# Edge blocks of a windowed attention, widened from 192 keys to 256 with zero weights

## The chip, the cores and the metric

One Trainium2 chip, one core of it. The metric is the device time of one execution in microseconds (us), the median of several runs. Below, PE is the matrix engine (TensorE) and PEld its loads of the stationary operand, DVE is VectorE, ACT is ScalarE, POOL is GpSimd and SP is SyncE, which issues most transfers.

## The reference

The program is one layer of a bidirectional encoder, on two requests of 256 and 2048 rows with width 1024. After a normalization and one input projection, the columns go two ways: 512 channels through a gated long convolution (Hyena, by Fourier transforms) and 8 heads of 64 through a dilated sliding-window attention. Both are normalized, joined, projected and added; a gated feed-forward network follows. The attention is what matters here:

```python
DILATED_BRANCHES = ((128, 1), (512, 4), (2048, 16))   # window, dilation
R = window // (2 * dilation)                          # 64 in all three
rel = jnp.arange(W)[None, :] - R - jnp.arange(b)[:, None]
valid = (jnp.abs(rel) <= R)[None] & ((key_pos >= 0) & (key_pos < Ls))[:, None, :]
s = jnp.where(valid, s + bias, NEG_INF)
p = jnp.exp(s - m)                                    # m: the row's maximum
den = jnp.sum(p, axis=-1)
o = jnp.einsum('brnhqk,brnkhe->brnqhe', p, v) / den
```

Each query sees the keys at most 64 steps (of the dilation) to either side, and a key in front of the sequence or behind it does not count. The three branches are then merged by their softmax denominators.

## The kernel before

The work is float32 throughout. Projections, the output product and the feed-forward network take three products of rounded halves each (the helper `mm3`, lines 208 to 210); attention and Hyena are woven into one stage, from about 985 to 1656 us of the profiled execution. The functions are generators: each `yield` hands the turn to the other one, and `weave` takes the one that is behind its share (the shares stand in `RATES`). That gives the order of the program. A scheduler then orders the instructions of each engine at build time, and each engine runs its list in that order.

`attention` goes over four pairs of heads, three branches for each, and the groups of blocks of `attention_groups`. A block is 128 queries of one pair of heads against its keys, and it takes four steps:

- `scores` (lines 906 and 907): two products for each head into the PSUM tile `aS`; then DVE adds the bias and takes the row's minimum (line 910; the sign is turned in the scores), and ACT takes the exponential (line 913), both on `aP`, a tile with two buffers.
- `flip` (line 922): PE transposes the weights `aP`, 128 keys at a time, into `aT`; the copy to `aPT` is made by DVE for each third block and by ACT for the others (line 926, or line 929 where the parts are not both 128 keys).
- `values` (line 938): for each head and part, the product of `aPT` and the values `aV`, summed in `aOp`. A column of ones beside the values gives the denominator. Each such float32 product is two PE instructions in the trace.
- At the end of a group, ACT copies `aOp` to `aO` (line 942) and SP stores it.

There are 216 blocks. Inside a sequence a block sees 256 keys, in two parts of 128. At its two ends a block sees 192: the first block of a sequence in parts of 64 and 128 keys, the last in parts of 128 and 64. There are 48 of these edge blocks: for each pair of heads 2 and 2 in the branch of dilation 1 and 8 in that of dilation 4. The other blocks (dilation 16, and the short request in the dilated branches) have one part of 128 keys. So in an edge block the value products of one part have 64 rows, and the transposes of that part have 64 columns. `attention_values` (lines 813 to 846) loads the values of a branch: half a tile for the first 64 keys, whole tiles of 128, and half a tile for the last 64; POOL writes the ones first (line 820).

The Hyena steps that run between have their PE products on lines 692, 693, 723, 727, 741 and 778. The addition on POOL (line 735) takes what DVE made on lines 731 to 734, and line 741 multiplies its result.

Of the kernel before, what the change touches and what calls it, by code (L numbers as in the profile page):

```python
# [15 lines left out]
AF = mybir.ActivationFunctionType  # L16
# [5 lines left out]
P = 128  # L22
# [167 lines left out]
class Hybrid:  # L190
# [624 lines left out]
    def attention_values(self, wp, b, cs):  # L815

        nc = self.nc
        dil = DILS[b]
        vo = wp.tile([P, 22, 130], F32, tag="aV", name="aV", bufs=2)
        nc.gpsimd.memset(vo[:, :, 0:130:129], 1.0)  # L820
        vt = vo[:, :, 1:129]
        av = self.tok["av"][:, cs]
        ld = lambda o, i: nc.sync.dma_start(out=o, in_=i)
        base = {}
        n = 0
        for r in (1, 0):
            off, L = REQ[r]
            base[r] = n
            ls = L // dil
            if ls >= 256:  # L830
                nb = ls // P
                e = 64 * dil
                ld(vt[0:64, n:n + dil], av[off:off + e].rearrange("(p s) k -> p s k", s=dil))
                if dil == 1:
                    ld(vt[:, n + 1:n + nb], av[off + e:off + L - e].rearrange("(c p) k -> p c k", p=P))
                else:
                    for c in range(1, nb):
                        o2 = off + e + (c - 1) * P * dil
# [35 lines left out]
    def attention(self, wp, psS, psT, psO, first, mq):  # L874
        nc, a = self.nc, self.a
        q1, q2 = [], []

        def scores(heads, g, i, blk, ot, bias, b):
            r, kind, _ = g
            res, j, nb = blk  # L880
            dil = DILS[b]
            off, L = REQ[r]
            ps = psS.tile([P, 2, 256], F32, tag="aS", name="aS")
            sb = wp.tile([P, 2, 256], F32, tag="aP", name="aP", bufs=2)
            for hh in range(2):
                Ql, Ks, Qh = heads[hh]
                t0 = off + res + dil * P * j
                qs = slice(t0, t0 + dil * (P - 1) + 1, dil)
                if kind == "win":
                    qa, qb = Qh[:, qs], Ql[:, qs]  # L890
                    k0 = max(0, P * j - 64)
                    n = min(nb * P, P * j + 192) - k0
                    v0, N = 0, n
                    b0 = k0 - (P * j - 64)
                    m0 = off + res + dil * k0
                    rhs = Ks[:, m0:m0 + dil * (n - 1) + 1:dil]
                elif kind == "res":
                    qa, qb = Qh[:, qs], Ql[:, qs]
                    e = res - res % 2
                    rhs = Ks[:, off:off + L].rearrange("p (j s) -> p s j", s=dil)[:, e:e + 2]  # L900
                    v0, n, N, b0 = P * (res % 2), P, 256, 0
                else:
                    qa, qb = Qh[:, off + j:off + L:2], Ql[:, off + j:off + L:2]
                    rhs = Ks[:, off:off + L].rearrange("p (j s) -> p s j", s=2)
                    v0, n, N, b0 = P * j, P, 256, 256 if b == 1 else 128
                nc.tensor.matmul(ps[:, hh, :N], qa, rhs, start=True, stop=False)
                nc.tensor.matmul(ps[:, hh, :N], qb, rhs, start=False, stop=True)
            for hh in range(2):
                mn = ot[:, i, 130 + hh:131 + hh]
                nc.vector.tensor_tensor_reduce(out=sb[:, hh, :n], in0=ps[:, hh, v0:v0 + n],  # L910
                                               in1=bias[:, hh, b0:b0 + n], scale=1.0, scalar=3e38,
                                               op0=ALU.add, op1=ALU.min, accum_out=mn)
                nc.scalar.activation(sb[:, hh, :n], sb[:, hh, :n], AF.Exp, scale=-1.0, bias=mn)
            return sb, n

        def flip(x):
            sb, n, first = x["sb"], x["n"], x["first"]
            ch = [(0, 64), (64, 128)] if first else [(0, P)] + ([(P, n - P)] if n > P else [])
            pt = psT.tile([P, 2, 2, P], F32, tag="aT", name="aT")
            for hh in range(2):  # L920
                for c, (c0, cn) in enumerate(ch):
                    nc.tensor.transpose(pt[:cn, hh, c], sb[:, hh, c0:c0 + cn], self.ident)  # L922
            pe = wp.tile([P, 2, 2, P], F32, tag="aPT", name="aPT", bufs=3)
            eng = nc.vector.tensor_copy if x["k"] % 3 == 0 else nc.scalar.copy
            if all(cn == P for _, cn in ch):
                eng(pe[:, :, :len(ch)], pt[:, :, :len(ch)])
            else:
                for c, (c0, cn) in enumerate(ch):
                    eng(pe[:cn, :, c], pt[:cn, :, c])
            x["pe"], x["ch"] = pe, ch  # L930

        def values(x):

            po, vt, i, pe, ch = x["po"], x["vt"], x["i"], x["pe"], x["ch"]
            for hh in range(2):
                hs = slice(65 * hh, 65 * hh + 65)
                for c, (c0, cn) in enumerate(ch):
                    nc.tensor.matmul(po[:, i, hs], pe[:cn, hh, c], vt[:cn, x["v"] + c * x["vs"], hs],  # L938
                                     start=(c == 0), stop=(c == len(ch) - 1))
            if x["last"]:  # L940
                n = i + 1
                nc.scalar.copy(x["ot"][:, :n, 0:130], po[:, :n])  # L942
                x["store"]()
# [30 lines left out]
        k = 0  # L974
# [4 lines left out]
        for hp in range(4):  # L979
# [6 lines left out]
            for b in range(3):  # L986
                dil = DILS[b]
                lo = (0, 256, 640)[b]
                w = (256, 384, 256)[b]
                bias = wp.tile([P, 2, 384], F32, tag="aB", name="aB", bufs=2)  # L990
                nc.sync.dma_start(out=bias[:, :, :w], in_=a["abias"][:, 2 * hp:2 * hp + 2, lo:lo + w])
                vt, vbase = self.attention_values(wp, b, cs)
                for g in self.attention_groups(b, (0, 1) if hp == 3 else (1, 0)):
                    r, kind, blks = g
                    ot = wp.tile([P, G, W], F32, tag="aO", name="aO", bufs=4)
                    po = psO.tile([P, G, 130], F32, tag="aOp", name="aOp")
                    for i, blk in enumerate(blks):
                        res, j, nb = blk
                        if hp == 0:
                            next(own, None)  # L1000
                        sb, n = scores(heads, g, i, blk, ot, bias, b)
                        x = dict(sb=sb, n=n, first=(kind == "win" and j == 0), k=k, po=po, vt=vt, i=i, ot=ot,
                                 last=(i == len(blks) - 1), store=store(b, hp, g, ot))
                        if kind == "win":
                            x["v"], x["vs"] = vbase[r] + j * dil + res, dil
# [680 lines left out]
```

## Time and profile before

| | |
|---|---|
| median of 3 runs | 3516.02 us (3508.4 to 3517.49) |
| the profiled execution | 3503.98 us |
| its span, first to last instruction | 3502.1 us |
| mean granted clock of TensorE | 0.970 |
| stage of attention and Hyena | 985 to 1656 us |
| the edge blocks' value products with 64 rows | 192 PE instructions |
| the edge blocks' transposes with 64 columns | 96 |

A row of the trace names the line, the engine and the operation, the tile written and the tiles read, and the shapes. For PE, `64*128` means that 64 rows and 128 columns of the array are in use. "Idle before" is the time in which the engine had nothing running ahead of these instructions, with what ended it. Products on PE overlap: the next one starts before the last has ended, so the time that one takes on PE is the distance from its start to the next start, not its length.

### The profile page before, as it was taken

The numbers are of one execution on the slowest core, as the hardware profiler recorded it, in microseconds if no ns is written. First come the engines' busy times: TensorE is split into PE (matmuls) and PEld (weight loads), VectorE is DVE, ScalarE is ACT, GpSimd is POOL, SyncE is SP. The second block draws the span as 40 slices with busy tenths as digits, with TensorE's granted clock in tenths as the row PEclk, the third lists the DMA queues.
The fourth block names the chain that finished last, engine by engine and source line by source line (L and its number), as shares of the span: only waits on it lengthen the run. The fifth ranks groups of instructions, "written<-read, shape, count | busy, mean of one in ns | idle before, by whom it ended". The sixth has DMA issues, their size and how long they took to land.

```text
span 3502.1 us, 56839 instructions
## 1 busy us (share of the span) xinstructions
PE 3290.7 (94%) x20926; PEld 3020.3 (86%) x20926; DVE 2461.5 (70%) x4254; ACT 1560.1 (45%) x2922; POOL 1267.1 (36%) x946
## 2 busy tenths in 40 slices
PE   7999899999989999999799899999999999899998
PEld 4877788788857786778799799999899999899998
DVE  7989878776575658644887766667767667457657
ACT  4576743333244545455554433334333334344443
POOL 1487761142232413110444433334533335123222
PEclk9999999999999999998999899999999999999999
DMA  6454457776585857593676523445444224456555
GB/s 244 133 169 135 148 182 234 238 263 219 177 246 160 243 163 216 157 272 106 185 225 184 193 96 122 145 158 187 179 158 146 85 95 148 173 190 229 206 190 172
DMA packets 408909, 628.02 MB, mean 179 GB/s; under 512 B 29007, under 2 KB 232015, under 8 KB 402711
## 3 DMA queue, kind: packets, MB, share of 16 engines
q1 hardware_dynamic: 355472, 593.13, 52.1%
q10 hardware_dynamic: 52072, 28.40, 2.7%
q8 instruction: 166, 2.72, 0.3%
q0 software_dynamic: 1088, 2.85, 0.2%
q14 instruction: 111, 0.91, 0.1%
HBM read 419.03 MB, written 205.25 MB: 178 GB/s over the span
## 4 chain that ended last, share of the span: by engine, by line
PE 42%; DVE 5%; DMA 2%; issue 2%; ACT 1%; POOL 1%; ACTq 0%; SPq 0%; DVEq 0%; POOLq 0%
PE w L210 9%; PE w L208 9%; PE w L209 9%; PE fd L210 4%; PE fd L209 4%; PE fd L208 4%; DVE fT L1251 1%; DMA hl<-d_opT 0%; DMA d_x1T<-ox 0%; DVE ohy L1159 0%; DVE ox L1214 0%; DVE hl L203 0%; POOL oat L1145 0%; PE om L208 0%; PE om L210 0%
## 5 line engine op out<-in xcount | busy, mean ns | idle before, releaser
L208 PE MATMUL w<-hh,whi 128*128 128x288 f32 (+1 forms) x2464 | 737.3, 300 | 13.1 <-ACT whi L1345 8.3
L210 PE MATMUL w<-hh,wlo 128*128 128x290 f32 (+1 forms) x2464 | 734.2, 299 | 13.7 <-POOL wlo L203 10.1
L209 PE MATMUL w<-hl,whi 128*128 128x288 f32 (+1 forms) x2464 | 737.2, 300 | 3.3 <-DVE hl L203 3.2
L210 PEld LDWEIGHTS w<-hh,wlo 128*128 128x128 f32 x2464 | 471.5, 192 | 15.7 <-POOL wlo L203 11.2
L208 PEld LDWEIGHTS w<-hh,whi 128*128 128x128 f32 x2464 | 472.2, 192 | 14.9 <-ACT whi L1345 8.6
L209 PEld LDWEIGHTS w<-hl,whi 128*128 128x128 f32 x2464 | 474.0, 192 | 4.6 <-DVE hl L203 4.4
L208 PE MATMUL pj<-hThi,wihi 128*128 128x386 f32 (+1 forms) x1152 | 403.4, 351 | 12.6 <-ACT u L629 5.2
L209 PE MATMUL pj<-hTlo,wihi 128*128 128x386 f32 (+1 forms) x1152 | 401.0, 348 | 7.4 <-DVE hTlo L203 7.4
L210 PE MATMUL pj<-hThi,wilo 128*128 128x386 f32 (+1 forms) x1152 | 402.8, 350 | 0.0
L208 PE MATMUL fd<-hh,dwh 128*128 128x288 f32 x1210 | 360.4, 298 | 12.6 <-ACT dwh L1551 12.6
L210 PE MATMUL fd<-hh,dwl 128*128 128x288 f32 x1210 | 359.3, 297 | 0.0
L209 PE MATMUL fd<-hl,dwh 128*128 128x288 f32 x1210 | 358.0, 296 | 0.0
L938 PEld LDWEIGHTS aOp<-aV,aPT 128*128 128x128 f32 (+1 forms) x1408 | 197.1, 199 | 57.8 <-issue 18.4
L208 PEld LDWEIGHTS pj<-hThi,wihi 128*128 128x128 f32 x1152 | 221.3, 192 | 28.0 <-issue 7.8
L209 PEld LDWEIGHTS pj<-hTlo,wihi 128*128 128x128 f32 x1152 | 221.6, 192 | 24.2 <-DVE hTlo L203 9.8
L208 PEld LDWEIGHTS fd<-hh,dwh 128*128 128x128 f32 x1210 | 230.2, 190 | 13.3 <-ACT dwh L1551 12.8
L735 POOL TENSOR_TENSOR ht<-ht,ht 128x512 f32<-128x512 f32 x72 | 102.7, 1427 | 381.9 <-DVE ht L734 298.1
L210 PEld LDWEIGHTS pj<-hThi,wilo 128*128 128x128 f32 x1152 | 221.0, 192 | 12.1 <-issue 7.8
L209 PEld LDWEIGHTS fd<-hl,dwh 128*128 128x128 f32 x1210 | 229.8, 190 | 0.4
L210 PEld LDWEIGHTS fd<-hh,dwl 128*128 128x128 f32 x1210 | 228.2, 189 | 0.1
L938 PE MATMUL aOp<-aV,aPT 128*128 128x65 f32 (+1 forms) x1408 | 213.1, 285 | 11.3 <-ACT aO L942 3.8
L910 DVE CUSTOM_DVE_ANT_0 aP<-aS,aB 128x256 f32<-128x256 f32 (+2 forms) x432 | 135.9, 354 | 120.7 <-PE aT L922 79.4
(297 smaller groups left out, 7860.7 us busy)
## 6 DMA issues: line engine op xcount, KB each, us to landing
hl<-d_G SPq DMA_DIRECT2D x154, 288.0 KB, 5.1
dwl<-d_S SPq DMA_DIRECT2D x59, 704.0 KB, 4.9
wiraw<-in_w_in SPq DMA_DIRECT2D x72, 512.0 KB, 4.7
d_G<-cv SPq DMA_DIRECT2D x42, 576.0 KB, 3.0
wraw<-in_w_gate SPq DMA_DIRECT2D x22, 1024.0 KB, 5.0
wraw<-in_w_up SPq DMA_DIRECT2D x22, 1024.0 KB, 4.8
adat<-in_ada_t SPq DMA_DIRECT2D x36, 512.0 KB, 5.4
d_fA<-fae SPq DMA_DIRECT2D x72, 256.0 KB, 2.6
```

The source lines that it names most:

```text
L208: mm(out, wh, xh, start=first, stop=False, skip_group_check=more)
L209: mm(out, wh, xl, start=False, stop=False, skip_group_check=more)
L210: mm(out, wl, xh, start=False, stop=last, skip_group_check=more)
L735: nc.gpsimd.tensor_tensor(out=t1, in0=t1, in1=t2, op=ALU.add)
L910: nc.vector.tensor_tensor_reduce(out=sb[:, hh, :n], in0=ps[:, hh, v0:v0 + n], in1=bias[:, hh, b0:b0 + n], scale=1.0, scalar=3e38, op0=ALU. ...
L938: nc.tensor.matmul(po[:, i, hs], pe[:cn, hh, c], vt[:cn, x["v"] + c * x["vs"], hs], start=(c == 0), stop=(c == len(ch) - 1))
L1251: v.tensor_tensor(out=o, in0=x, in1=y, op=ALU.subtract)
```

## The change

An edge block is handled as one of 256 keys. Its scores stay as they are, with 192 keys. The tile `aP` is used in its full width: the 64 columns that belong to no key (the first 64 of a first block, the last 64 of a last one) are set to zero by POOL, and the 192 weights stand in the others. All transposes then have 128 columns and all value products 128 rows. The values of the first 64 keys are loaded into rows 64 to 127 of their tile instead of 0 to 63, and POOL fills the unused half of a tile with ones, so that zero weights meet finite numbers. The copy of `aPT` becomes one instruction for each block.

```diff
@@ attention_values
-                ld(vt[0:64, n:n + dil], av[off:off + e].rearrange("(p s) k -> p s k", s=dil))
+                nc.gpsimd.memset(vo[0:64, n:n + dil], 1.0)
+                nc.gpsimd.memset(vo[64:P, n + nb * dil:n + (nb + 1) * dil], 1.0)
+                ld(vt[64:P, n:n + dil], av[off:off + e].rearrange("(p s) k -> p s k", s=dil))
@@ scores
+            s0 = 0
+            if n == 192:
+                s0 = b0
+                nc.gpsimd.memset(sb[:, :, 0:s0] if s0 else sb[:, :, n:256], 0.0)
             for hh in range(2):
                 mn = ot[:, i, 130 + hh:131 + hh]
-                nc.vector.tensor_tensor_reduce(out=sb[:, hh, :n], in0=ps[:, hh, v0:v0 + n],
+                e = sb[:, hh, s0:s0 + n]
+                nc.vector.tensor_tensor_reduce(out=e, in0=ps[:, hh, v0:v0 + n],
...
-                nc.scalar.activation(sb[:, hh, :n], sb[:, hh, :n], AF.Exp, scale=-1.0, bias=mn)
-            return sb, n
+                nc.scalar.activation(e, e, AF.Exp, scale=-1.0, bias=mn)
+            return sb, 1 if n == P else 2
@@ flip
-            ch = [(0, 64), (64, 128)] if first else [(0, P)] + ([(P, n - P)] if n > P else [])
...
-                for c, (c0, cn) in enumerate(ch):
-                    nc.tensor.transpose(pt[:cn, hh, c], sb[:, hh, c0:c0 + cn], self.ident)
+                for c in range(n):
+                    nc.tensor.transpose(pt[:, hh, c], sb[:, hh, P * c:P * c + P], self.ident)
...
-            if all(cn == P for _, cn in ch):
-                eng(pe[:, :, :len(ch)], pt[:, :, :len(ch)])
-            else:
-                for c, (c0, cn) in enumerate(ch):
-                    eng(pe[:cn, :, c], pt[:cn, :, c])
+            (nc.vector.tensor_copy if x["k"] % 3 == 0 else nc.scalar.copy)(pe[:, :, :n], pt[:, :, :n])
@@ values
-                for c, (c0, cn) in enumerate(ch):
-                    nc.tensor.matmul(po[:, i, hs], pe[:cn, hh, c], vt[:cn, x["v"] + c * x["vs"], hs],
+                for c in range(n):
+                    nc.tensor.matmul(po[:, i, hs], pe[:, hh, c], vt[:, x["v"] + c * x["vs"], hs],
```

The number of PE instructions is the same. DVE loses 21 copies and ACT 27; POOL gains 48 zero fills of `aP` and 24 fills of `aV`.

On PE, before, in the first pair of heads where one sequence of the dilation-4 branch ends and the next begins (a last edge block is transposed, then a first one; `aS` are scores, `aT` transposes, `aOp` value products):

```order
L906 MATMUL aS<-Ks,Qh 128x256 [waits DVE_49]
L907 MATMUL aS<-Ks,Ql 128x256
L906 MATMUL aS<-Ks,Qh 128x256
L907 MATMUL aS<-Ks,Ql 128x256
L922 MATMUL aT<-ident,aP 128x128 [waits PE_49,Activation_49]
L922 MATMUL aT<-ident,aP 64x128
L922 MATMUL aT<-ident,aP 128x128 [waits Activation_49]
L922 MATMUL aT<-ident,aP 64x128
L938 MATMUL aOp<-aV,aPT 128x65 [waits DVE_49]
L938 MATMUL aOp<-aV,aPT 128x65 x3
L906 MATMUL aS<-Ks,Qh 128x256 [waits DVE_49]
L907 MATMUL aS<-Ks,Ql 128x256
```

On PE, after the change, at the same place:

```order
L908 MATMUL aS<-Ks,Qh 128x256 [waits DVE_49]
L909 MATMUL aS<-Ks,Ql 128x256
L908 MATMUL aS<-Ks,Qh 128x256
L909 MATMUL aS<-Ks,Ql 128x256
L928 MATMUL aT<-ident,aP 128x128 [waits PE_49,Activation_49]
L928 MATMUL aT<-ident,aP 128x128 [waits Pool_49]
L928 MATMUL aT<-ident,aP 128x128 [waits Activation_49]
L928 MATMUL aT<-ident,aP 128x128
L939 MATMUL aOp<-aV,aPT 128x65 [waits DVE_49]
L939 MATMUL aOp<-aV,aPT 128x65 x3
L908 MATMUL aS<-Ks,Qh 128x256 [waits DVE_49]
L909 MATMUL aS<-Ks,Ql 128x256
```

The order is the same here; the transposes of 64 columns have become 128 wide, and a transpose waits for POOL. In the whole program 42 transposes have such a wait.

On POOL, before, in the same stretch (`ht` is the Hyena addition of line 735, `Ks` the rounding of the next heads' keys, `hS` of Hyena's gate):

```order
L203 TENSOR_TENSOR Ks<-Ks,kh 64x576 [waits DMAHW6_49,Activation_49,Pool_49]
L735 TENSOR_TENSOR ht_8116<-ht_8116,ht_8117 128x512 [waits DVE_49,PE_49,Pool_49]
L735 TENSOR_TENSOR ht_8211<-ht_8211,ht_8212 128x512 [waits DVE_49,PE_49]
L735 TENSOR_TENSOR ht_8235<-ht_8235,ht_8236 128x512 [waits DVE_49,PE_49]
L820 MEMSET aV 128x22x2 [waits DMAHW0_49,PE_49]
L735 TENSOR_TENSOR ht_8323<-ht_8323,ht_8324 128x512 [waits DVE_49,Pool_49]
L735 TENSOR_TENSOR ht_8342<-ht_8342,ht_8343 128x512 [waits DVE_49,Pool_49]
L203 TENSOR_TENSOR hS<-hg,hS 64x512 [waits DMAHW0_49,DMAHW2_49,DVE_49,DMAHW4_49,PE_49,Pool_49]
```

On POOL, after the change:

```order
L203 TENSOR_TENSOR Ks<-Ks,kh 64x576 [waits DMAHW6_49,Activation_49,Pool_49]
L913 MEMSET aP 128x2x64 [waits PE_49,Activation_49,Pool_49]
L913 MEMSET aP 128x2x64 [waits PE_49,Activation_49]
L735 TENSOR_TENSOR ht_8116<-ht_8116,ht_8117 128x512 [waits DVE_49]
L735 TENSOR_TENSOR ht_8211<-ht_8211,ht_8212 128x512 [waits DVE_49]
L913 MEMSET aP 128x2x64 [waits PE_49,Activation_49,Pool_49] x2
L735 TENSOR_TENSOR ht_8235<-ht_8235,ht_8236 128x512 [waits DVE_49]
L820 MEMSET aV 128x22x2 [waits DMAHW0_49,PE_49]
L735 TENSOR_TENSOR ht_8323<-ht_8323,ht_8324 128x512 [waits DVE_49,Pool_49]
L913 MEMSET aP 128x2x64 [waits PE_49,Activation_49,Pool_49] x2
L735 TENSOR_TENSOR ht_8342<-ht_8342,ht_8343 128x512 [waits DVE_49]
L913 MEMSET aP 128x2x64 [waits PE_49,Activation_49,Pool_49] x4
```

The fills stand between the Hyena additions in POOL's list, and each waits until PE has transposed the block that used the buffer before.

## Rows read from the trace of the kernel before

**Rows 1.** The page: busy time, share of the span and instructions of each engine.

```profile
PE 3290.7 (94%) x20926; PEld 3020.3 (86%) x20926; DVE 2461.5 (70%) x4254; ACT 1560.1 (45%) x2922; POOL 1267.1 (36%) x946
```

**Rows 2.** The stage of attention and Hyena as one stretch: length, then busy times.

```profile
core 0: us, PE busy (x) PEld busy (x) DVE busy (x) ACT busy (x) POOL busy (x), PEclk, DMA share, GB/s
985.00:1656.00 671.00, 636.23 (x3432) 501.68 (x3432) 419.68 (x1350) 347.95 (x828) 162.76 (x124) 0.95 0.67 195
```

**Rows 3.** Waits of PE in that stage: us in total, times, longest.

```profile
PE aS L906 <- DVE aO L910: 5.9, 4, 4.1
...
PE aT L922 <- ACT aP L913: 4.9, 8, 1.8
...
PE hs L741 <- POOL ht L735: 1.5, 1, 1.5
```

**Rows 4.** Groups by shape in that stage, products and loads: busy us, mean ns, idle.

```profile
L938 PE MATMUL aOp<-aV,aPT 64*128 64x65 f32 x192 | 42.2, 300 | 2.1 <-DVE aPT L929 2.1
L922 PE MATMUL aT<-ident,aP 128*64 128x128 f32 x96 | 25.1, 283 | 0.2 <-ACT aP L913 0.2
...
L922 PEld LDWEIGHTS aT<-ident,aP 128*128 128x128 f32 x608 | 82.1, 152 | 26.4 <-ACT aP L913 10.4 <-issue 8.2 <-ACT aO L942 2.4
...
L922 PEld LDWEIGHTS aT<-ident,aP 128*64 128x64 f32 x96 | 11.2, 117 | 5.3 <-issue 2.7 <-ACT aP L913 1.7
```

**Rows 5.** PE in order of time, 1080 to 1090 us: start, length, what.

```profile
1079.99 1.53 PE L938 MATMUL aOp<-aV,aPT 64*128 64x65 f32 x8
1081.35 1.08 PE L741 MATMUL hs<-ht,htab 128*128 128x512 f32 x2
1082.26 1.00 PE L938 MATMUL aOp<-aV,aPT 128*128 128x65 f32 x8
1083.10 0.61 PE L922 MATMUL aT<-ident,aP 128*128 128x128 f32 x4
...
1086.42 0.62 PE L922 MATMUL aT<-ident,aP 128*64 128x128 f32 x4
1086.88 1.02 PE L741 MATMUL hs<-ht,htab 128*128 128x512 f32 x2
1087.74 1.42 PE L938 MATMUL aOp<-aV,aPT 128*128 128x65 f32 x8
1089.09 0.55 PE L906 MATMUL aS<-Ks,Qh 128*128 128x192 f32 x1
```

**Rows 6.** Groups by shape in that stage: the copies from `aT`.

```profile
L926 DVE COPY aPT<-aT 128x512 f32<-128x512 f32 x26 | 17.8, 686 | 14.1 <-PE aT L922 14.0
...
L929 DVE COPY aPT<-aT 128x256 f32<-128x256 f32 x21 | 8.7, 414 | 7.0 <-PE aT L922 6.8
L929 DVE COPY aPT<-aT 64x256 f32<-64x256 f32 x21 | 8.6, 409 | 4.6 <-PE aT L922 4.6
...
L926 ACT COPY aPT<-aT 128x512 f32<-128x512 f32 x62 | 36.1, 583 | 47.0 <-PE aT L922 46.4
...
L929 ACT COPY aPT<-aT 128x256 f32<-128x256 f32 x27 | 10.0, 369 | 24.3 <-PE aT L922 24.3
L929 ACT COPY aPT<-aT 64x256 f32<-64x256 f32 x27 | 9.8, 364 | 5.9 <-PE aT L922 5.9
```

**Rows 7.** Groups by shape on POOL: the Hyena addition, and two fills elsewhere.

```profile
L735 POOL TENSOR_TENSOR ht<-ht,ht 128x512 f32<-128x512 f32 x44 | 59.8, 1359 | 180.2 <-DVE ht L734 138.9 <-PE aOp L938 23.0 <-PE aT L922 6.9
...
L424 POOL MEMSET acc<- 128x512 f32 x4 | 2.1, 540 | 7.6 <-PE fnr L457 7.6
...
masks.py:197 POOL MEMSET ident<- 128x128 f32 x1 | 0.2, 204 | 0.3 <-POOLq L1675 0.3
```

**Rows 8.** Groups by shape in that stage: an edge block's steps on DVE and ACT.

```profile
L910 DVE DVE_READ_ACCUMULATOR2_ANT aO<- 128x1 f32 x432 | 35.2, 82 | 0.0
...
L910 DVE CUSTOM_DVE_ANT_0 aP<-aS,aB 128x192 f32<-128x192 f32 x96 | 30.0, 352 | 25.0 <-issue 11.0 <-ACT aO L942 5.1 <-DMA d_O<-aO 3.5
...
L913 ACT ACTIVATE aP<-aP,aO 128x192 f32<-128x192 f32 x96 | 38.5, 448 | 19.7 <-DVE aO L910 18.3 <-PE hs2z L727 1.2
```

More of the change, by code (lines that the diff above doesn't have):

```diff
@@ L911, in scores @@
                                                in1=bias[:, hh, b0:b0 + n], scale=1.0, scalar=3e38,
                                                op0=ALU.add, op1=ALU.min, accum_out=mn)
-                nc.scalar.activation(sb[:, hh, :n], sb[:, hh, :n], AF.Exp, scale=-1.0, bias=mn)
-            return sb, n
+                nc.scalar.activation(e, e, AF.Exp, scale=-1.0, bias=mn)
+            return sb, 1 if n == P else 2
         def flip(x):
-            sb, n, first = x["sb"], x["n"], x["first"]
@@ L918, in flip @@
-            ch = [(0, 64), (64, 128)] if first else [(0, P)] + ([(P, n - P)] if n > P else [])
+            sb, n = x["sb"], x["n"]
             pt = psT.tile([P, 2, 2, P], F32, tag="aT", name="aT")
             for hh in range(2):
-                for c, (c0, cn) in enumerate(ch):
-                    nc.tensor.transpose(pt[:cn, hh, c], sb[:, hh, c0:c0 + cn], self.ident)
+                for c in range(n):
+                    nc.tensor.transpose(pt[:, hh, c], sb[:, hh, P * c:P * c + P], self.ident)
@@ L923, in flip @@
             pe = wp.tile([P, 2, 2, P], F32, tag="aPT", name="aPT", bufs=3)
-            eng = nc.vector.tensor_copy if x["k"] % 3 == 0 else nc.scalar.copy
-            if all(cn == P for _, cn in ch):
-                eng(pe[:, :, :len(ch)], pt[:, :, :len(ch)])
-            else:
-                for c, (c0, cn) in enumerate(ch):
-                    eng(pe[:cn, :, c], pt[:cn, :, c])
-            x["pe"], x["ch"] = pe, ch
+            (nc.vector.tensor_copy if x["k"] % 3 == 0 else nc.scalar.copy)(pe[:, :, :n], pt[:, :, :n])
@@ L932, in values @@
+            x["pe"] = pe
         def values(x):
-            po, vt, i, pe, ch = x["po"], x["vt"], x["i"], x["pe"], x["ch"]
+            po, vt, i, pe, n = x["po"], x["vt"], x["i"], x["pe"], x["n"]
             for hh in range(2):
                 hs = slice(65 * hh, 65 * hh + 65)
-                for c, (c0, cn) in enumerate(ch):
-                    nc.tensor.matmul(po[:, i, hs], pe[:cn, hh, c], vt[:cn, x["v"] + c * x["vs"], hs],
-                                     start=(c == 0), stop=(c == len(ch) - 1))
+                for c in range(n):
+                    nc.tensor.matmul(po[:, i, hs], pe[:, hh, c], vt[:, x["v"] + c * x["vs"], hs],
+                                     start=(c == 0), stop=(c == n - 1))
@@ L1001, in attention @@
                         sb, n = scores(heads, g, i, blk, ot, bias, b)
-                        x = dict(sb=sb, n=n, first=(kind == "win" and j == 0), k=k, po=po, vt=vt, i=i, ot=ot,
+                        x = dict(sb=sb, n=n, k=k, po=po, vt=vt, i=i, ot=ot,
                                  last=(i == len(blks) - 1), store=store(b, hp, g, ot))
```

## The prediction

> **What bounds the kernel now.** I read the busy shares first: PE has work in 94% of the span, its weight loads in 86%, DVE in 70%, ACT in 45% and POOL in 36% [rows 1]. Then I cut out the one stage that the change touches, 985 to 1656 us, as a single stretch: of its 671.0 us PE is busy for 636.2 (94.8%), DVE for 419.7, ACT for 348.0 and POOL for 162.8 [rows 2]. So PE bounds this stage too, with 34.8 us of idle time. But a busy PE is not a PE that streams without a break, and its weight loads are busy for only 501.7 us, 75% of the stage: I keep these two shares as the bounds of how firmly PE sets the pace. The waits come third: the longest of PE on the attention's own chain are 5.9 us for DVE's minimum and 4.9 us for ACT's exponential [rows 3]. They are small, so time that is taken off PE should mostly come off the stage. Last I looked at PE in order of time around edge blocks, which is where the price of 64 rows is seen.
>
> **The value products.** The eight instructions of an edge block whose first part has 64 rows start at 1079.99 and the next product starts at 1081.35: they hold PE for 1.36 us. An edge block whose second part has 64 rows starts at 1087.74 and gives way at 1089.09: 1.35 us. Eight instructions that all have 128 rows go from 1082.26 to 1083.10: 0.84 us [rows 5]. The same number of columns (65) streams through in all of them. So a block with 64-row parts costs 1.355 - 0.84 = 0.515 us more, although half of its products have half the rows. With 192 instructions of 64 rows, four for each block, there are 48 such blocks [rows 4]: 48 x 0.515 = 24.7 us of PE time go away, in a stage where PE is busy 94.8%.
>
> The Trainium skill has a rule for it, in "TensorEngine Tiling (Array Packing)", section Key Properties: going from one tiling mode to another, not merely to another tile, drains TensorE; 64 rows are such a mode beside 128. The trace agrees with it for the rows, with the 0.515 us above. By the same list of modes 128x64 is one as well, so the 64-column transposes should drain too; that makes a rival, below.
>
> **The transposes.** 96 of them grow from 64 columns to 128. The load of the stationary side gets longer, from a mean of 117 ns to 152 [rows 4], 96 x 35 ns = 3.4 us of PEld time. But four transposes with 64-column parts take 0.62 us, and four of full width 0.61 us [rows 5]: the load lies beside the product ahead of it. I cost this at nothing; the cover is the streaming of the 128 columns, and without it the price would be the 3.4 us.
>
> By the Trainium skill, "TensorE: Matmul & The Clock Gate", section on LDWEIGHTS, a load takes a time in proportion to its columns and its rows do not matter. It speaks against the change: an estimate from it is 128/1.2 - 64/1.2 = 53 ns for each, 5.1 us in all, with nothing back for the rows. The trace shows 35 ns instead, hidden.
>
> **The copies.** On ACT two copies of 0.369 and 0.364 us become one of 0.583, 27 times: 27 x 0.150 = 4.1 us less. On DVE 0.414 and 0.409 become 0.686, 21 times: 2.9 us less [rows 6]. Both engines have room (348 and 420 of 671 us), and PE's work covers them, so I cost these 7.0 us at nothing; where a value product waits for the copy, it comes some 0.15 us earlier. From zero to 7.0 us of gain are the bounds.
>
> **The fills on POOL.** None of this shape in the stage before. A fill of 128x128 took 0.204 us and one of 128x512 0.540 us [rows 7]. The 48 fills of aP have 128 elements in each partition: 48 x 0.204 = 9.8 us. Of the 24 fills of aV, 16 have 130 elements (0.204 each, 3.3 us) and 8 have 520 (0.540 each, 4.3 us). POOL's busy time goes from 162.8 to about 180 us of the stage, no bound. The transfers of values keep their number and size and only land in other partitions; SP's list keeps them as they were.
>
> What matters is the new wait. The transposes of an edge block wait for the fill; behind a waiting transpose stands everything on PE. The fill needs the buffer that the transposes two blocks earlier give free, and that is also what DVE's work on the block needs. From there the block takes 2 x (0.352 + 0.082) us on DVE and, at least partly behind it, 2 x 0.448 us on ACT [rows 8], 1.76 us when added up. A fill that finds POOL in the middle of a Hyena addition is done after at most 1.36 + 0.20 = 1.56 us [rows 7], still inside that. So a POOL that works does not make the transposes late; only one that is itself held by a wait does. The lower bound of the cost is zero. The upper one is the fill behind an addition that waits for DVE: POOL sat idle for 180.2/44 = 4.1 us before each of these, mostly for DVE [rows 7]. Less the 1.76 us that is 2.3 us for each block so placed, 112 us were it all 48. I take it near the lower bound, 1.5 us in total: the additions' inputs in POOL's list after the change come from products that stand well ahead of the transposes in question in PE's. In the other direction the additions stand behind fills that wait for PE. PE waited only 1.5 us for an addition in the whole stage [rows 3], so these have room.
>
> **The sum.** Of the 24.7 us the share that reaches the end lies between 75% and 95% by the two busy shares of the stage; I take the lower one, since edge blocks often stand where the next transposes wait for an exponential, which does not come earlier: 18.5 us. Less 1.5 us for the fills, 17 us. The profiled execution took 3503.98 us and would take 3487. It lies 12 us under the median of 3516.02, so the same 17 us make the median 3499. After the stage nothing of the work is changed; it starts earlier.
>
> **The rivals.** *Absorbed.* The edge blocks get shorter on PE, but PE then waits for the exponential of the next block, whose chain starts at scores that PE issued ahead of the products in question. For it: the waits of 5.9 and 4.9 us stand just there [rows 3], and the loads are busy only 75%. Against it: 94.8% busy, and behind the three groups of products shown the next one follows without a gap [rows 5]. A quarter to a third of the gain would be left, some 6 us: 3510.
>
> *Everything counts.* The stage is held by PE and by the turn-around of its buffers, so the 24.7 us come in full and the shorter copies too: 24.7 + 7.0 = 32 us, 3484. Against it: waits of PE exist at all.
>
> *Transposes drain as well.* If changing the columns held PE like changing the rows, the 48 blocks would give another 24.7 us: twice 18.5, less 1.5, is 35.5 us, 3480. It is the case of the second mode in the rule of "TensorEngine Tiling". The row of 0.62 against 0.61 us [rows 5] speaks plainly against it.
>
> *Slower: the fill comes late.* POOL's list is fixed, so a fill that stands behind a Hyena addition waits with it for DVE. With 2.3 us for each such block it decides from 18.5/2.3 = 8 of the 48 blocks on; with 18 of them the cost is 41 us, less 18.5 makes 23 us slower: 3539. For it: POOL's 180 us of idle time in front of these additions [rows 7]. Against it: DVE's list puts the Hyena work in the same order among the blocks, so the addition is usually done by then.
>
> **How the numbers follow.** The forecast, 12 to 23 us faster, has a chance of 0.50; absorbed 0.27; everything counts 0.10; transposes drain 0.02; the late fill 0.11. A difference under 0.3%, 10.5 us, cannot be told from none with this kernel. Faster by more than that: 0.50 + 0.10 + 0.02 = 0.62. Slower: 0.09 of the late fill; the other 0.02 of it and absorbed make 0.29 for the same. The likeliest case alone spans 3493 to 3504; the range takes in everything counts at one end and the absorbed case with a little loss at the other: 3484 to 3517.
>
> **What would show it.** Right: no value product with 64 rows is left, eight value products hold PE for 0.84 us in each block, and the stretch from the first score to the end of line 942's copies is some 17 us shorter, with the later stages as long as before. The fills show 0.2 us each, and PE hardly waits for POOL in front of a transpose. Wrong: PE's waits for ACT or DVE in the stage grow by more than 10 us (absorbed), waits for POOL's fill appear on PE (late fill), or the groups of eight products stay near 1.35 us, which would mean that the 64 rows were not their price.

## The result: 41 us faster, 8 us below the forecast's range

Measured on one chip: 3476.09 us after (median of four runs, 3468.71 to 3479.78) against 3516.76 before (four runs, 3508.4 to 3523.95); the ratio is 0.9883, 95% interval 0.9855 to 0.991. The forecast was 3499 with a range of 3484 to 3517: right in direction, wrong in size. The two profiled executions took 3475.70 and 3503.98 us, 28.3 apart; that the medians are 40.7 apart is part of the story below.

The page after (answers to [rows 1]):

```profile
PE 3256.6 (94%) x20926; PEld 3001.6 (86%) x20926; DVE 2459.5 (71%) x4233; ACT 1559.7 (45%) x2895; POOL 1279.4 (37%) x1018
```

Three stretches of the kernel before: first score to last value product, from there to the first product of the gate and up projections, and these projections (columns as in [rows 2]):

```profile
990.00:1655.40 665.40, 631.92 (x3427) 499.83 (x3426) 415.60 (x1343) 346.49 (x825) 161.28 (x123) 0.96 0.67 195
1655.40:1933.30 277.90, 237.65 (x1892) 232.26 (x1891) 214.27 (x437) 142.46 (x307) 126.15 (x107) 0.94 0.67 204
1933.30:2968.90 1035.60, 1013.90 (x7394) 1008.97 (x7395) 721.77 (x980) 389.32 (x740) 419.33 (x331) 0.98 0.40 141
```

The same three of the kernel after:

```profile
994.80:1633.00 638.20, 602.64 (x3428) 485.31 (x3426) 413.79 (x1322) 344.07 (x798) 175.83 (x195) 0.97 0.69 203
1633.00:1912.80 279.80, 240.00 (x1891) 234.64 (x1890) 214.34 (x437) 142.45 (x307) 126.10 (x107) 0.93 0.67 202
1912.80:2941.30 1028.50, 1009.85 (x7394) 1006.04 (x7395) 721.05 (x980) 389.77 (x740) 418.10 (x331) 0.99 0.40 142
```

The attention stage is 27.2 us shorter, and the gate and up stage, in which no instruction was changed, 7.1 us. The clock column rose in both (0.96 to 0.97 and 0.98 to 0.99); between them it is 0.94 and 0.93.

PE in order of time after the change (answers to [rows 5]: start, length, what):

```profile
1084.75 1.00 PE L939 MATMUL aOp<-aV,aPT 128*128 128x65 f32 x8
1085.59 0.60 PE L928 MATMUL aT<-ident,aP 128*128 128x128 f32 x4
1086.03 1.00 PE L939 MATMUL aOp<-aV,aPT 128*128 128x65 f32 x8
1086.84 0.58 PE L908 MATMUL aS<-Ks,Qh 128*128 128x256 f32 x1
...
1090.21 1.00 PE L939 MATMUL aOp<-aV,aPT 128*128 128x65 f32 x8
1091.03 0.52 PE L908 MATMUL aS<-Ks,Qh 128*128 128x192 f32 x1
```

Eight value products now hold PE for 0.81 to 0.84 us in the blocks shown (1084.75 to 1085.59, 1086.03 to 1086.84, 1090.21 to 1091.03). The last of them is the edge block that starts at 1087.74 in [rows 5] and held PE for 1.35 us there. The groups by shape in the stage (answer to [rows 4, 6, 7]):

```profile
L939 PE MATMUL aOp<-aV,aPT 128*128 128x65 f32 x1408 | 188.6, 278 | 15.3 <-ACT aPT L930 6.6 <-DVE aPT L930 4.6 <-ACT aO L943 2.7
L928 PE MATMUL aT<-ident,aP 128*128 128x128 f32 x704 | 126.3, 281 | 4.9 <-ACT aP L920 4.9
L930 ACT COPY aPT<-aT 128x512 f32<-128x512 f32 x89 | 51.8, 583 | 70.7 <-PE aT L928 70.3
L930 DVE COPY aPT<-aT 128x512 f32<-128x512 f32 x47 | 32.3, 686 | 25.0 <-PE aT L928 24.9
L913 POOL MEMSET aP<- 128x128 f32 x48 | 9.8, 206 | 141.2 <-PE aT L928 124.3 <-ACT aO L943 15.7 <-ACT aP L920 1.2
```

No product of 64 rows and no transpose of 64 columns is left. The 48 fills last 206 ns each and wait for PE, as POOL's order after the change, ahead of the prediction, shows them queued. The waits of PE in the stage (answer to [rows 3]):

```profile
PE aOp L939 <- ACT aPT L930: 6.6, 11, 3.3
PE aT L928 <- ACT aP L920: 4.9, 6, 2.0
PE aS L908 <- DVE aO L917: 4.8, 2, 4.0
...
PE aOp L939 <- DVE aPT L930: 4.6, 8, 1.6
PE hs L741 <- POOL ht L735: 3.4, 4, 1.2
```

No row has PE waiting for a fill. Its wait for the Hyena addition, which stands behind fills, grew from 1.5 to 3.4 us. What grew most is PE's wait for the copies `aPT`, from 6.1 us before, in the three rows that follow, to 11.2 us after (6.6 and 4.6):

```profile
PE aOp L938 <- ACT aPT L926: 3.3, 6, 1.8
...
PE aOp L938 <- DVE aPT L929: 2.1, 1, 2.1
...
PE aOp L938 <- DVE aPT L926: 0.7, 2, 0.4
```

PE's idle time in the stage, by the stretches above, went from 33.5 us (665.40 - 631.92) to 35.6 (638.20 - 602.64).

### The profile page after: what moved, and what is told of

Read it like the earlier page. It is cut to its first block, busy times and chain, and to the rows that moved or that the text cites. A ratio compares the mean times of both kernels' runs of the same rounds, so it can differ in the third digit from the quotient of the medians.

```text
span 3473.9 us, 56909 instructions
## 1 busy us (share of the span) xinstructions
PE 3256.6 (94%) x20926; PEld 3001.6 (86%) x20926; DVE 2459.5 (71%) x4233; ACT 1559.7 (45%) x2895; POOL 1279.4 (37%) x1018
## 4 chain that ended last, share of the span: by engine, by line
PE 42%; DVE 5%; DMA 2%; issue 2%; ACT 1%; POOL 1%; SPq 0%; ACTq 0%; DVEq 0%; POOLq 0%
PE w L210 9%; PE w L208 9%; PE w L209 9%; PE fd L210 5%; PE fd L209 5%; PE fd L208 5%; DVE fT L1252 1%; DMA hl<-d_opT 0%; DMA d_x1T<-ox 0%; DVE ohy L1160 0%; DVE ox L1215 0%; PE om L208 0%; POOL oat L1146 0%; PE om L209 0%; PE om L210 0%
## 5 line engine op out<-in xcount | busy, mean ns | idle before, releaser
L208 PE MATMUL w<-hh,whi 128*128 128x288 f32 (+1 forms) x2464 | 735.6, 299 | 13.2 <-ACT whi L1346 8.4
L210 PE MATMUL w<-hh,wlo 128*128 128x290 f32 (+1 forms) x2464 | 733.5, 299 | 11.2 <-POOL wlo L203 7.0
L210 PEld LDWEIGHTS w<-hh,wlo 128*128 128x128 f32 x2464 | 470.4, 191 | 13.2 <-POOL wlo L203 8.0
L208 PEld LDWEIGHTS pj<-hThi,wihi 128*128 128x128 f32 x1152 | 220.2, 191 | 28.3 <-issue 7.8
L208 PEld LDWEIGHTS fd<-hh,dwh 128*128 128x128 f32 x1210 | 230.0, 190 | 13.2 <-ACT dwh L1552 12.8
L939 PEld LDWEIGHTS aOp<-aV,aPT 128*128 128x128 f32 x1408 | 184.3, 198 | 48.8 <-issue 18.4
L203 POOL TENSOR_TENSOR wlo<-ws,whi 128x512 fp32r<-128x512 f32 x88 | 131.6, 1495 | 232.3 <-ACT whi L1346 225.4
L203 POOL TENSOR_TENSOR hl<-hl,hh 128x576 fp32r<-128x576 f32 (+1 forms) x66 | 116.1, 1766 | 264.6 <-ACT hh L1494 191.4
```

Of the source, the lines that this page charges most:

```text
L203: eng.tensor_tensor(out=lo, in0=x, in1=hi.bitcast(F32), op=ALU.subtract)
L208: mm(out, wh, xh, start=first, stop=False, skip_group_check=more)
L210: mm(out, wl, xh, start=False, stop=last, skip_group_check=more)
L939: nc.tensor.matmul(po[:, i, hs], pe[:, hh, c], vt[:, x["v"] + c * x["vs"], hs], start=(c == 0), stop=(c == n - 1))
```

## The experiments

Theory at the start: the 64-row value products are the cost, and PE's time sets the pace. Rivals: the transposes, the copies, the order of the program, the clock, the turn-around of buffers. The table collects all runs. Each ratio is to runs of the kernel before made beside that kernel; the columns of the stages and "low" are of one profiled execution each; the first row has those of the first profile of before. "Changes" is the number of changes between 64 and 128 rows in an edge block; the clock is the median over the timed runs; "low" is the time at the lower of TensorE's two levels (1.2 of 2.4 GHz) in the attention stage of the profiled execution, summed from the trace's clock records. "At 0.970" moves the median to one mean clock by 1.9 us for each 0.001, which is the slope over the 51 runs of the kernel before made beside the experiments (3505 to 3529 us at 0.961 to 0.972). That is bookkeeping: it tells how much of a difference goes along with the clock, not what caused it, and it carries the slope of one kernel over to the others, a little beyond the range in which it was found.

| kernel | changes | median us | ratio [95%] | clock | at 0.970 | attention stage | low | gate/up |
|---|---|---|---|---|---|---|---|---|
| before, 51 runs | 4 | 3514.1 | 1 | 0.968 | 3510 | 665.4 | 58 | 1035.6 |
| before_again | 4 | 3519.42 | 1.0009 [0.9994, 1.0025] | 0.9675 | 3515 | 673.5 | 80 | 1034.9 |
| wide_transposes | 4 | 3516.89 | 1.0012 [0.9998, 1.0027] | 0.9675 | 3512 | 680.8 | 90 | 1035.1 |
| extra_narrow | 4 | 3524.54 | 1.0024 [1.0011, 1.0037] | 0.9665 | 3518 | 683.1 | 66 | 1027.5 |
| before_three | 4 | 3491.79 | 0.9931 [0.9916, 0.9945] | 0.970 | 3492 | 653.2 | 59 | 1035.6 |
| by_part | 2 | 3489.36 | 0.9925 [0.9906, 0.9943] | 0.9725 | 3494 | 648.8 | 45 | 1028.8 |
| wide_last | 4 or 0 | 3487.10 | 0.9921 [0.99, 0.9942] | 0.973 | 3493 | 646.9 | 33 | 1029.1 |
| after_extra | 0 | 3490.11 | 0.993 [0.9911, 0.9948] | 0.975 | 3500 | 655.0 | 41 | 1029.8 |
| after | 0 | 3476.09 | 0.9883 [0.9855, 0.991] | 0.9735 | 3483 | 638.2 | 44 | 1028.5 |
| after_again | 0 | 3476.95 | 0.9894 [0.9876, 0.9911] | 0.9715 | 3480 | 643.3 | 53 | 1027.0 |
| wide_values | 0 | 3473.80 | 0.9885 [0.9866, 0.9903] | 0.974 | 3481 | 639.6 | 32 | 1028.3 |
| after_three | 0 | 3461.16 | 0.9845 [0.9823, 0.9866] | 0.973 | 3467 | 624.7 | 49 | 1028.1 |
| values_three | 0 | 3453.50 | 0.9822 [0.9806, 0.9837] | 0.974 | 3461 | 621.4 | 28 | 1027.4 |

**Both kernels again** (before_again and after_again, no edit).

> The kernel before, unchanged, for a second profile and more times. Theory 'all of PE's time comes through' (the 24.7 us of the 64-row products reach the end in full, and a little of the clock beside them; the rest of the 40.7 us is that the executions of before lie between 3504 and 3524): the second profile has its stage of attention near 666 us and a span of 3500 to 3520, the ratio is 1.000 within 0.003. Rival 'the change also speeds up other stages': the second profile shows the stages after the attention as long as the first one did, 1035.7 us for the gate and up products and 518.4 for the down products, so that the 7 us that these lost after the change are the change's.

> The changed kernel, unchanged, for a second profile and more times on one chip with the others. Theory 'all comes through': ratio 0.990 (0.988 to 0.993), the attention's stage 636 to 641 us long against 666, the later stages like those of before within their own spread. Rival 'the change also speeds up other stages': ratio 0.988 or lower, the gate and up products at 1028 us again against 1036 for before.

The gate and up stage came out as the rival had it, 1034.9 us before and 1027.0 after, so the 7 us belong to the change. The attention stages were longer than the theory said, 673.5 us for 666 and 643.3 for 636 to 641, and the ratio of 0.9894 lies between the two forecasts. The kernel before spreads over 24 us in its twelve runs (3507.22 to 3531.33), the one after over 8 us in six (11 us in the four of the first comparison). The first profile of before, at 3503.98, was thus a quick execution, while that of after was an ordinary one: profiles alone show 28 us, medians 36 to 41.

**Transposes and copies alone** (wide_transposes):

```diff
-                    nc.tensor.transpose(pt[:cn, hh, c], sb[:, hh, c0:c0 + cn], self.ident)
+                    nc.tensor.transpose(pt[:, hh, c], sb[:, hh, c0:c0 + P], self.ident)
...
+            eng(pe[:, :, :len(ch)], pt[:, :, :len(ch)])
```

> Only the transposes are widened to 128 columns and the two copies of an edge block made one; the value products keep their 64 rows. (The last blocks' 64 free columns are set to zero; the first blocks transpose neighbouring keys as filling, so no fill there.) Theory 'the 64 rows are the price': ratio 0.997 to 1.001, eight value products of an edge block still hold PE 1.35 us. Rival 'the shorter copies and single transposes bring part of it': ratio 0.994 to 0.996, some 15 us of gain without any change of the rows. Rival of the prediction 'transposes drain as well': 24 us, 0.993.

The value products keep their 64 rows; POOL fills the free columns of last blocks only. Eight value products of an edge block still hold PE for 1.37 us:

```profile
1077.79 1.53 PE L936 MATMUL aOp<-aV,aPT 64*128 64x65 f32 x8
1079.16 1.08 PE L727 MATMUL hs2z<-hx,htab 128*128 128x512 f32 x2
```

Nothing comes of it: 1.0012. The 128-column transposes and the single copies are no part of the gain.

**Value products alone** (wide_values):

```diff
+                    if cn < P:
+                        nc.gpsimd.memset(pe[cn:P, :, c], 0.0)
...
-                    nc.tensor.matmul(po[:, i, hs], pe[:cn, hh, c], vt[:cn, x["v"] + c * x["vs"], hs],
+                    nc.tensor.matmul(po[:, i, hs], pe[:, hh, c], vt[:, x["v"] + c * x["vs"], hs],
```

> Only the value products are widened to 128 rows: transposes keep 64 columns, the copies stay two, and POOL sets the free half of the copied tile to zero. Theory 'the 64 rows are the price': ratio 0.990 to 0.993, like the whole change, eight value products at 0.81 to 0.84 us in all blocks. Rival 'the shorter copies bring part of it': ratio 0.994 to 0.996, about half of the gain missing.

Eight value products of an edge block mostly take 0.81 to 0.86 us here, as in the other blocks; one of 128 and 64 keys:

```profile
1085.83 1.00 PE L942 MATMUL aOp<-aV,aPT 128*128 128x65 f32 x8
1086.64 0.52 PE L908 MATMUL aS<-Ks,Qh 128*128 128x192 f32 x1
```

All of the gain comes: 0.9885, with the two copies of each edge block kept. So the value products are where the whole gain starts.

**Half of the blocks** (wide_last: as above, in the last block of each sequence only; `first` blocks keep 64 rows).

> Value products widened to 128 rows in the 24 last blocks only; the 24 first blocks keep their 64 rows. Theory 'PE time counts in full': half of the PE time, 11 to 12 us, plus 7 us in the feed-forward stage, whose order in this program is that of the changed kernel, plus some of the clock: ratio 0.993 to 0.996. Rival 'the gain is not in proportion to the 64-row products': 0.990 or 0.998.

Half of the edit gave more than half of the gain, 0.9921, below the range that was expected. One reason is the gate and up stage, which takes 1029.1 us as after the whole change. Another goes along with the clock: 33 us at the lower level in the attention stage against 58.

**The same PE time, without 64 rows** (after_extra: the kernel after, with two products more in each edge block, which nothing reads):

```diff
+            if x["edge"]:
+                for c in range(2):
+                    nc.tensor.matmul(x["spare"], pe[:, c, c], vt[:, x["v"] + c * x["vs"], 0:65], start=True, stop=True)
```

> The changed kernel with two more value products of 128 rows in each of the 48 edge blocks, into 65 spare columns that nothing reads: 48 x 4 x 112 ns = 21.5 us of PE time, about what the 64 rows cost before (24.7), but with 128 rows. Theory 'PE time counts in full in this stage, and the 64 rows also lower the clock': the stage gets 21 to 23 us longer, 662 to 666 us, with less time at the low clock than before (32 to 53 us in the three runs with 128 rows, 58 to 90 in the three with 64); ratio to before 0.994 to 0.997, so about a third of the change's gain is left. Rival, the prediction's three quarters: stage 656 us or less, ratio 0.993 or lower. Rival 'only PE time counts, the clock is chance': the low clock takes 58 us or more again, stage 670 us.

PE in order of time, where the four added instructions follow a block's eight:

```profile
1074.95 1.00 PE L939 MATMUL aOp<-aV,aPT 128*128 128x65 f32 x8
1075.79 0.61 PE L943 MATMUL aOp<-aV,aPT 128*128 128x65 f32 x4
1076.23 0.60 PE L928 MATMUL aT<-ident,aP 128*128 128x128 f32 x4
```

They hold PE for 0.44 us, some 21 us in 48 blocks, and the median rose by 13.2 to 14.0. Read alone this says that about 65% of PE's time reaches the end, and the figures are those of the rival with the prediction's three quarters: a stage of 655.0 us and a ratio of 0.993. But the kernel ran at the highest clock of all, 0.975; at equal clock it is 18 us slower than after (the mean of its two rows), 87%. The higher share thus rests on the step to equal clock. The theory was right on the clock: 41 us at the lower level, not 58 or more.

**The changes of rows without the PE time they replace** (extra_narrow: the kernel after, with a product of 64 rows and one column behind each head's; each is two instructions):

```diff
+                if x["edge"]:
+                    nc.tensor.matmul(x["spare"][:, hh:hh + 1], pe[:64, hh, hh], vt[:64, x["v"] + hh * x["vs"], 0:1],
+                                     start=True, stop=True)
```

> The changed kernel, with two further products in each of the 48 edge blocks, one after each head's, of 64 rows and a single column, into spare columns that nothing reads. It brings back four changes between 128 and 64 rows for each block and nearly no columns. PE's own time: four changes at some 90 ns and four short instructions, about 0.5 us for each block, 24 us in all, about what the 64-row products of the kernel before cost. Theory 'the changes of rows also cost clock': low-clock time in the attention stage back at 58 to 90 us, the stage at 665 us or more, time about 3510 to 3518, ratio 0.998 to 1.001. Rival 'only PE's own time counts, the clock went for another reason' (as with the two further products of 128 rows): low-clock time 32 to 53 us, stage 653 to 658, about 3490, ratio 0.993.

```profile
1073.75 0.56 PE L939 MATMUL aOp<-aV,aPT 128*128 128x65 f32 x4
1074.24 0.38 PE L942 MATMUL aOp<-aV,aPT 64*128 64x1 f32 x2
1074.55 0.66 PE L939 MATMUL aOp<-aV,aPT 128*128 128x65 f32 x4
1075.14 0.38 PE L942 MATMUL aOp<-aV,aPT 64*128 64x1 f32 x2
1075.44 0.60 PE L908 MATMUL aS<-Ks,Qh 128*128 128x256 f32 x1
```

The edge block now takes 1.69 us (1073.75 to 1075.44) against 0.84: I had sized the addition at 0.5 us, and it is 0.85, 41 us in all. That error of size covers the time beyond the expected 3518. The clock is the point: with four changes for each block it is 0.9665, the lowest of all, where after_extra had 0.975. At equal clock this kernel is 37 us slower than after (the mean of its two rows again), 90% of its 41 us; the other 10 or so go along with the clock. At the lower level its stage spent 66 us, as the theory had it. The stage in the two kernels, after_extra first, with the clock third from the end:

```profile
992.30:1647.30 655.00, 621.91 (x3620) 506.63 (x3618) 414.70 (x1322) 345.39 (x798) 176.22 (x195) 0.97 0.68 198
```

```profile
995.30:1678.40 683.10, 649.07 (x3619) 525.64 (x3618) 416.29 (x1324) 346.54 (x799) 177.21 (x195) 0.95 0.65 190
```

**Half of the changes, the 64 rows kept** (by_part: the kernel before, with a block's products ordered by part, so that those of 64 rows stand together; the sums of the two heads are then open in one bank at a time and the first is not kept whole, so it is read for its times only):

```diff
-            for hh in range(2):
-                hs = slice(65 * hh, 65 * hh + 65)
-                for c, (c0, cn) in enumerate(ch):
+            for c, (c0, cn) in enumerate(ch):
+                for hh in range(2):
+                    hs = slice(65 * hh, 65 * hh + 65)
```

> The kernel before with the eight value products of a block ordered by part, both heads' 64-row products side by side: two changes between 64 and 128 rows in a block instead of four, with the same 64 rows. Theory 'each change of rows costs some 90 ns, and each further 64-row product behind another one some 50': an edge block's eight products take 1.36 - 2 x 0.09 + 0.05 = 1.22 us, 6 us less in the stage. The order in the feed-forward stage is that of the changed kernel here too, so by the theory 'the order there is worth 7 us' the gate and up products take 1028 us against 1035 and the ratio is 0.996 to 0.997; without it 0.998 to 0.999. Rival 'only the changes cost': eight products 1.10 us, ratio 0.995 or with the order 0.993.

```profile
1075.84 1.25 PE L938 MATMUL aOp<-aV,aPT 64*128 64x65 f32 x8
1076.92 1.08 PE L727 MATMUL hs2z<-hx,htab 128*128 128x512 f32 x2
```

Eight products take 1.08 us, between 0.84 and 1.355, although four of them still have 64 rows: the change of rows is the price, not the 64 rows. Two changes cost 0.24 us here and four cost 0.515 in the kernel before, 120 to 130 ns for each. By single instructions, from start to next start at the higher clock: 202 ns where 64 rows give way to 128 and 205 where 128 give way to 64, then 161 ns between the two instructions behind the change, whichever rows they have, where otherwise 112 ns pass between two of 128 rows. Two of 64 rows that don't follow a change stand 112 ns apart as well, so the 50 ns that the theory put on the 64 rows belong to the change, and its rival "only the changes cost" (1.10 us, 0.993) is borne out. The ratio is 0.9925, where the theory had 0.996 to 0.997; the clock, 0.9725 against 0.968, was in neither.

**More buffers** (after_three, before_three and values_three: after, before and wide_values with three buffers of `aP` and two of `aPT`, instead of two and three):

```diff
-            sb = wp.tile([P, 2, 256], F32, tag="aP", name="aP", bufs=2)
+            sb = wp.tile([P, 2, 256], F32, tag="aP", name="aP", bufs=3)
...
-            pe = wp.tile([P, 2, 2, P], F32, tag="aPT", name="aPT", bufs=3)
+            pe = wp.tile([P, 2, 2, P], F32, tag="aPT", name="aPT", bufs=2)
```

> The changed kernel with three buffers of the weights aP and two of their transposed copy instead of two and three. Theory 'PE sets the pace': no gain, ratio like the change within 0.002 (0.988 to 0.992). Rival 'the turn-around of aP's two buffers holds the stage': faster than the change by 5 us or more, 0.987 or lower. Slower is open, since the copies lose a buffer.

> The kernel before with three buffers of aP and two of aPT, instead of two and three; products of 64 rows as they were. Theory 'the buffers' turn-around is a cost of its own': about the same 15 us come off as from the changed kernel, 3498 to 3503, ratio 0.995 to 0.997. Rival 'it counts only once PE's 64-row products are gone, because PE sets the pace until then': under 5 us, ratio 0.999 to 1.001. In the other direction, a gain of more than 20 us would mean that the turn-around hid behind the 64-row products and is the larger cost.

> The kernel before with value products of 128 rows alone (transposes of 64 columns, two copies as before, the unused rows of aPT set to zero by POOL), and three buffers of aP, two of aPT. Theory 'the wide transposes and the single copy are worth nothing': the same time as the changed kernel with these buffers, 3461 +- 5, ratio 0.983 to 0.986. Rival 'with only two buffers of aPT the zero fill on POOL sits between the copy and the products and is late': 5 to 15 us more, ratio 0.987 to 0.989, with waits of PE's value products for POOL.

The theory "PE sets the pace" falls in part here. All three gain: 15.8 us on after_again, 22 on before, 20.3 on wide_values. On before that is more than the 15 us expected and more than the 20 named there as a sign that the buffers' turn-around is the larger cost; it is not, since with three buffers the wide products still bring 31 us (after_three) and 38 (values_three). The wait that goes is DVE's for a free `aP`, until the transposes two blocks back are done; it is the same in the kernel before (the first fence) as it nearly vanishes in before_three (the second):

```profile
DVE aP L910 <- PE aT L922: 79.4, 53, 4.8
```

```profile
DVE aP L910 <- PE aT L922: 13.3, 16, 2.1
```

The stage of before_three:

```profile
992.90:1646.10 653.20, 622.41 (x3428) 492.43 (x3426) 411.89 (x1341) 343.97 (x824) 162.61 (x123) 0.95 0.68 199
```

Against the kernel before, PE has the same products, and its busy time falls by 9.5 us (631.92 to 622.41), its idle time only by 2.7. So PE's busy time holds hidden waiting, most likely because a product that nothing follows closely is counted in its full length. The gains are nearly additive, and values_three is the fastest kernel of the study: 3453.50 us, 0.9822 [0.9806, 0.9837], faster than both kernels of the case and a little below the range that was expected. Whether it truly beats after_three (0.9845 [0.9823, 0.9866]) the intervals leave open; the rival of a late zero fill there is refuted.

**The gate and up stage.** POOL's list from there on is one and the same in after and in the other eight rows of the table whose stage takes 1027 to 1030 us, and another one, the same too, in before, before_again, wide_transposes and before_three with 1035. The two differ in one place, an exchange of an addition `gs` with a weight rounding `wlo`, 7 to 10 us ahead of the rounding shown below; the lists of DVE and ACT differ more. No run exchanges only this, so that the order is the cause is argued from the split of the rows and from the trace. POOL in order of time, before (last bracket: idle before, and what ended it):

```profile
1999.12 0.80 POOL L1423 TENSOR_TENSOR gs<-us,cv 128x286 f32<-128x286 f32 x1 [4.31 <-DVE us L1422]
1999.89 1.28 POOL L203 TENSOR_TENSOR wlo<-ws,whi 128x512 fp32r<-128x512 f32 x1
```

and after:

```profile
1970.55 2.75 POOL L1424 TENSOR_TENSOR gs<-us,cv 128x286 f32<-128x286 f32 x3 [0.59 <-DVE us L1423]
1973.26 1.30 POOL L203 TENSOR_TENSOR wlo<-ws,whi 128x512 fp32r<-128x512 f32 x1
```

Before, the rounding stands behind an addition that waits 4.31 us for DVE; after, behind one that waits 0.59. PE's wait for it, among its waits in the stage's first 80 us, is there before and gone after:

```profile
PE w L210 <- POOL wlo L203: 3.0, 1, 3.0
```

In before the lower clock sets in during this wait, which ends at 2001.2 us, and lasts from 2000.5 to 2007.4. The other three profiles with this order have the same wait, of 2.8 to 4.0 us, and a stretch at the lower clock about half as long. Fifteen us around that place, before and after:

```profile
1993.30:2008.30 15.00, 11.96 (x69) 11.73 (x68) 8.75 (x17) 3.90 (x9) 4.42 (x5) 0.77 0.63 225
```

```profile
1972.80:1987.80 15.00, 15.00 (x113) 15.00 (x113) 10.96 (x20) 5.01 (x12) 4.35 (x4) 1.00 0.53 189
```

44 products fewer fit into the same 15 us, at 0.13 us each 5.8 us: that is most of the stage's 7 us in this pair of profiles, about half of it the wait itself and half the clock. Why DVE's input comes late there was not followed further.

## Why the prediction was wrong, by its own steps

**Right: the place and the price.** Eight products of an edge block fell from 1.355 to 0.81 to 0.86 us, 48 times [rows 4, 5]: the 24.7 us are there. The transposes and copies, costed at nothing, are worth nothing (wide_transposes, wide_values). The Trainium skill states a drain at a change of tiling mode in "TensorEngine Tiling (Array Packing)", section Key Properties; by_part agrees with it for the rows, at 120 to 130 ns for each change. For the columns wide_transposes shows no such price, and that rival is refuted.

**Mis-sized: the share that reaches the end.** I took 75%, from the busy share of the loads, and got 18.5 us. The two kernels with added PE time give 87% and 90% at equal clock: about 22 us. Without the step to equal clock after_extra gives some 65% and extra_narrow more than its whole 41 us, so the share is less firm than the price. The waits for the exponential, my reason for the lower share, stand in the stage after the change as before (4.9 us in both; like the 5.9 us they are sums of several waits, not single ones as I wrote), so "absorbed" did not come that way. What grew is PE's wait for the copies, by 5.1 us, which I had expected to shrink.

**About right: the fills.** Forecast 1.5 us of loss through PE waiting for fills. PE does not wait for one; it waits 1.9 us longer for an addition behind them. POOL's busy time rose by 14.6 us (161.3 to 175.8) where some 17 were forecast.

**Failed: "After the stage nothing of the work is changed; it starts earlier."** The instructions are the same, but the scheduler orders the whole program at once, and the later order moved with the edit. The gate and up stage went from 1035 to 1027 to 1030 us, so that some 7 us were put at nothing here, and "the later stages as long as before", named as a sign of being right, did not come. I had compared the order around the edge blocks and not behind the stage.

**Left out: the clock.** No term of the sum had it. With four changes for each of 48 edge blocks the mean clock is 0.9665 to 0.970, in all seven sets of runs; with fewer, 0.9715 to 0.975, in all eight rows. It does not go in proportion: wide_last and by_part, with half the changes, stand at 0.973 and 0.9725, like after. Between before and after that is 0.0035 to 0.0055, by 1.9 us for each 0.001 some 7 to 10 us. In the profiled stages it is 58 to 90 us at the lower level against 28 to 53. after_extra and extra_narrow show that the lower clock comes with the changes and not with more work on PE alone. What in them does it, the empty stretches at each change or the short products, the runs do not separate.

Together: 22 of PE's time, 7 of the order and 7 to 10 of the clock make 36 to 39 us, against 38 by the 51 runs of before and 41 by the four of the first comparison. The forecast had 17 of them: 5 are missing in PE's time and the fills, the rest lies in the two terms that were put at nothing. The last two overlap: in the gate and up stage the profiles with before's order spend 32 to 37 us at the lower level and the others 17 to 30, worth 2 to 3 us by the same slope, which are in both. So the sum fits no better than to some 3 us. The same terms fit two kernels from which the 88% were not taken, at equal clock: for wide_last 24 x 0.515 x 0.88 + 7 = 17.9 us below before, measured 3510 - 3493 = 17; for by_part 48 x 0.275 x 0.88 + 7 = 18.6, measured 16.

**The range.** Its lower end of 3484 came from "everything counts", 32 us. That case put 7.0 us on the copies, which gave nothing, and knew neither of the two terms outside of PE's work. Its time was near for the wrong reason.

## What to carry to other kernels

Count the changes of rows on PE, not the rows in use: padding to full height can be cheaper than half the work, and so can grouping what has the same height. When a scheduler orders the whole program, compare its order behind the changed stage too, on every engine, and look there for stalls of PE, since the clock can fall with them, as here to 0.77 over 15 us. And a busy share of 95% does not prove that an engine is the only bound: a third buffer took another 16 to 22 us from this stage without touching a product.

## What the runs showed of the hardware that was not expected

- A change between 64 and 128 rows costs 120 to 130 ns for such products (202 to 205 ns from start to start at the change and 161 behind it, against 112), while 64-row products apart from changes keep the 112 ns.
- A change between 64 and 128 columns adds nothing that shows: four transposes with 64-column parts hold PE for 0.46 us (1086.42 to 1086.88) [rows 5], four of 128 columns for 0.44 (1085.59 to 1086.03, after), and widening all 96 left the time at 1.0012 of before.
- The mean clock goes along with the changes of rows: 0.9665 (extra_narrow) against 0.975 (after_extra), though both only add products to the same kernel.
- A wait of 3.0 us on PE in a dense stage came with a stretch at the lower clock: 0.77 over 15 us, against 1.00 where the wait is gone.
